# A hybrid recurrence and convolution block: the recurrent branch without GpSimd arithmetic, one-row products joined, the last filter layer stacked

## Chip, cores and metric

The kernel runs on one core of a Trainium2 chip. The metric is the device time of one execution in microseconds (us). Engines are named as the profile names them: PE (TensorE, products), PEld (its weight loads), DVE (VectorE), ACT (ScalarE), POOL (GpSimd), SP (DMA issue).

## The reference

One layer on 512 tokens of width 1024, in float32:

```
h   = x + Mixer(rmsnorm(x));  h = h + PEER(rmsnorm(h));  out = rmsnorm(h)
Mixer: proj = xn @ w_in, cut into q, zf_fwd, zf_bwd, inp, og, (x0, x1, v), gates
 A, 8 heads of 128: f = lb + (1-lb)*sigmoid(zf), k = (1-lb)*sigmoid(-zf), q = silu(q)
    S_t = diag(f_t) S_{t-1} + k_t inp_t^T,  o_t = S_t^T q_t   forward and reversed, summed
    y_a = (rmsnorm(o) * silu(og)) @ w_branch_a
 B, 1024 channels: width-3 convolution of x0, x1, v;  u = v*x1
    filters = (sin(sin(features) ...) @ filt_w3) * exp(-t*|decay|), forward and backward
    y_b = (x0 * (two-sided FFT convolution of u with the filters + bias*u)) @ w_branch_b
 out = (sigmoid(g_a)*y_a + sigmoid(g_b)*y_b) @ w_out
PEER: 8 heads choose 16 of 128^2 experts per token; sum of gelu(x.u_e)*g_e*v_e
```

## The kernel before

Float32 accuracy is had from fp32r products: an operand is split into `hi` (a cast by ACT, L85) and `lo = x - hi` (a subtraction, L86, on DVE unless the call names `nc.gpsimd`), and `mm3` issues hi*hi (L93), a product with the other operand's `lo` (L94) and one with its own (L95). `proj` loads 128 columns of a weight as `wraw` (128x1024), splits them into `whi` and `wlo`, two buffers, and sums 24 products of 512 columns in one of three PSUM banks `ps_mm`. Here L94 takes `xl, whi` and L95 takes `xh, wlo`.

The program has these stages: norm and turn of x to about 30 us; `hyena` to about 330, in four quarters of 256 channels; gates and projection of branch B to about 395; `hgrn`, 8 heads, to about 785; then `w_a`, `w_o` and PEER.

`hyena`: per quarter the projected rows are convolved, folded, transposed and split; the filter is made by two sine layers (once) and a last layer of 64 rows (`hid2`, `fw3`, L448, plain float32); both go through cosine and sine matrices as `mm3` sums (`ft`). The middle and the Nyquist element are single rows: `um`, `fm0`, `fm1` and `YN`, each as a hi and a lo tile of one row, enter a sum by two products with the row `alt` (L382 and L383, and others like them, 12 pairs in a quarter).

`hgrn`: `scores(hd)` scans the logarithms `lf` (L619) to `Z` on DVE (L628, L629), forms `EZ` and `E0` (L648 to L653), transposes `EZ` on PE (L662), builds the states `S`, and for 7 levels takes differences `Dt` (L689, L690), their exponential (ACT, L691), products `KM` (L692 to L694), a PE product (L698) and a masked copy into `sct` (L699). Beside it `weave` runs `project(hd+1)`: four projections, those with odd j split on POOL; then `sigmoids(hd+1)` and `values(hd+1)`, whose weights are split on POOL. Two more operations stand on POOL: `ksum` (L633) and the gating product of `so` (L621). The order within each engine comes from the framework's scheduler, not from the order of the code alone: each engine works its list in order, and a wait holds what stands behind it.

Of the kernel before, what the change touches and what calls it, by code (L numbers as in the profile page):

```python
# [21 lines left out]
P = 128  # L22
# [159 lines left out]
def turn(C, xn, xh, xl, tb):  # L182

    nc = C.nc
    ts_ = slice(tb * P, tb * P + P)
    for half in range(2):
        pt = C.ps_x.tile([P, 512], F32, name="ps_x")
        for j in range(4):
            k = half * 4 + j
            nc.tensor.transpose(pt[:, j * P : j * P + P], xn[:, k * P : k * P + P], C.ident)  # L190
        ks = slice(half * 4, half * 4 + 4)
        split(nc, xh[:, ks, ts_], xl[:, ks, ts_], pt.rearrange("p (j t) -> p j t", j=4))


FIRST_CONV = (8, 16)
# [107 lines left out]
def hyena(C, ctx, xh, xl, raws, fill):  # L303
# [9 lines left out]
    FH = 64  # L313
    NJ = HC // P
    H = L // 2

    first = dict(zip(FIRST_CONV, proj_halves(C, (None, None), xh, xl, raws=raws)))

# [5 lines left out]
        nc.vector.scalar_tensor_tensor(dst[:, : L - 1], ps[:, 1:], vcol(C, "cw2", blk), dst[:, : L - 1], op0=ALU.mult, op1=ALU.add)  # L324

    dft = {}
    hid2 = cp.tile([FH, L], F32, name="hid2")
    alt = cp.tile([1, H + 2], F32R, name="alt")
    altc = cp.tile([P, 1], F32R, name="altc")

    def setup(once):

        for name, w in (("ce", H + 2), ("so", H), ("co", H), ("se", H), ("coT", H), ("soT", H + 2)):
            hi = cp.tile([P, 2, w], F32R, name=name + "h")
            lo = cp.tile([P, 2, w], F32R, name=name + "l")
            for t in range(2):
                raw = once.tile([P, L], F32, name="dftraw", tag="ow", bufs=3)[:, :w]
                nc.sync.dma_start(raw, a[name][:, t])
                split(nc, hi[:, t], lo[:, t], raw)
            dft[name] = (hi, lo)  # L340
        raw = once.tile([P, L], F32, name="dftraw", tag="ow", bufs=3)
        nc.sync.dma_start(raw[:1, : H + 2], a["alt"])
        nc.sync.dma_start(raw[:, H + 2 : H + 3], a["altc"])
        nc.scalar.copy(alt, raw[:1, : H + 2])
        nc.scalar.copy(altc, raw[:, H + 2 : H + 3])


        zT = w2.tile([P, L], F32, name="zT", tag="x1")[:33]
        nc.sync.dma_start(zT, a["zT"])
        fw1 = once.tile([33, FH], F32, name="fw1")  # L350
        nc.sync.dma_start(fw1, a["f_w1"])
        fw2 = once.tile([FH, FH], F32, name="fw2")
        nc.sync.dma_start(fw2, a["f_w2"])

        def sine_layer(dst, ps, b, q):

            arg = once.tile([P, L], F32, name="arg", tag="ow", bufs=3)[:FH]
            kf = once.tile([P, L], F32, name="kf", tag="ow", bufs=3)[:FH]
            nc.vector.tensor_scalar(arg, ps, vcol(C, b)[:FH], vcol(C, q)[:FH], op0=ALU.add, op1=ALU.mult)
# [12 lines left out]
        ps = C.ps_x.tile([P, L], F32, name="ps_x")
        nc.tensor.matmul(ps[:FH], fw2, hid1, start=True, stop=True)
        sine_layer(hid2, ps[:FH], "f_b2", "f_q2")

    def ft(dst, mat, fb, src, mid=None):

        mh, ml = dft[mat]
        sl = slice(fb * P, fb * P + P)
        mm3(nc, dst, [((mh[:, t, sl], ml[:, t, sl]), (src[0][:, t], src[1][:, t])) for t in range(2)], stop=mid is None)  # L380
        if mid is not None:
            nc.tensor.matmul(dst, alt[:, sl], mid[0], start=False, stop=False)  # L382
            nc.tensor.matmul(dst, alt[:, sl], mid[1], start=False, stop=True)  # L383

    def nyquist(dst, src, mid):

        for t in range(2):
            nc.tensor.matmul(dst, altc, src[0][:, t], start=(t == 0), stop=False)
            nc.tensor.matmul(dst, altc, src[1][:, t], start=False, stop=False)
        nc.tensor.matmul(dst, alt[:, 0:1], mid[0], start=False, stop=False)  # L390
        nc.tensor.matmul(dst, alt[:, 0:1], mid[1], start=False, stop=True)

    def psum(w=HC):
        return C.ps_x.tile([P, L], F32, name="ps_x")[:, :w]
# [1 line left out]
    def hl(pool, shape, name, **kw):  # L396
        tag = kw.pop("tag", name)
        return (pool.tile(shape, F32R, name=name + "h", tag=tag + "h", **kw),
                pool.tile(shape, F32R, name=name + "l", tag=tag + "l", **kw))

    for half in range(D // HC):
        x0 = cp.tile([P, NJ, L], F32, name="x0")
        u = cp.tile([P, NJ, L], F32, name="u")
        us = hl(cp, [P, 2, HC], "us")
        ud = hl(cp, [P, 2, HC], "ud")
        um = hl(cp, [1, HC], "um")
        for j in range(NJ):
            cb = half * NJ + j
            x1 = w2.tile([P, L], F32, name="x1")
# [16 lines left out]
                split(nc, dst[0][:, :, js], dst[1][:, :, js], pt[:, q * HC : q * HC + HC].rearrange("p (t c) -> p t c", t=2))  # L426
            pm = psum(P)
            nc.tensor.matmul(pm[:1], uj[:, H : H + 1], C.ident, start=True, stop=True)
            split(nc, um[0][:, js], um[1][:, js], pm[:1])
            conv(x0[:, j], cb)  # L430
        if half == 0:
            with tc.tile_pool(name="hyo", bufs=1, side="right") as once:
                setup(once)

        fw3 = w2.tile([FH, 2, HC], F32, name="fw3", bufs=1)
        nc.scalar.dma_start(fw3, a["f_w3"].rearrange("f (d c) -> f d c", d=2)[:, :, half * HC : half * HC + HC])
        decb = w2.tile([P, 2, HC], F32, name="decb", bufs=1)
        for dr in range(2):
            o = dr * D + half * HC
            nc.scalar.dma_start(decb[:, dr], a["f_decay"][:, o : o + HC].to_broadcast([P, HC]))  # L440
        nc.scalar.activation(decb, decb, AF.Abs)
        pm_ = w2.tile([P, 2, 4, HC], F32, name="pm", bufs=1)
        for t in range(TB):
            win = w2.tile([P, 2, HC], F32, name="win")
            nc.scalar.activation(win, decb, AF.Exp, scale=vcol(C, "negt", t))
            ps = psum(2 * HC)
            for dr in range(2):
                nc.tensor.matmul(ps[:, dr * HC : dr * HC + HC], hid2[:, t * P : t * P + P], fw3[:, dr], start=True, stop=True)  # L448
            nc.vector.tensor_mul(win, ps.rearrange("p (d c) -> p d c", d=2), win)
            if t == 0:  # L450
                nc.vector.memset(win[0:1, 1], 0.0)
            nc.vector.tensor_add(pm_[:, 0, t], win[:, 0], win[:, 1])
            nc.vector.tensor_sub(pm_[:, 1, t], win[:, 0], win[:, 1])
        mid = []
        for q in range(2):
            m = hl(cp, [1, HC], f"fm{q}")
            split(nc, m[0], m[1], pm_[0:1, q, 2])
            mid.append(m)
        nc.vector.memset(pm_[0:1, :, 2], 0.0)
        fold = []  # L460
        for q in range(2):
# [82 lines left out]
def hgrn(C, ctx, xh, xl, ya, ga):  # L544
# [33 lines left out]
    def project(hd):  # L578

        raw = w2.tile([P, 4, L], F32, name="raw")  # L580
        for j, blk in enumerate((8 + hd, 16 + hd, hd, 32 + hd)):
            ps = proj(C, a["w_in"][blk], xh, xl, nc.gpsimd if j % 2 else None)
            nc.scalar.copy(raw[:, j], ps)
            yield
        st[hd] = [raw]

    def values(hd):
        ps = proj(C, a["w_in"][24 + hd], xh, xl, nc.gpsimd)
        vT = w1.tile([P, L], F32, name="vT")
        nc.scalar.copy(vT, ps)  # L590
        st[hd].append(vT)
# [747 lines left out]
```

## Time and profile before

| | |
|---|---|
| median of 3 runs | 2204.7 us (2198.98 to 2210.33) |
| profiled execution | 2201.49 us; span 2199.7; mean granted clock 0.989 |
| PE, DVE, ACT, POOL busy | 96%, 77%, 43%, 38% of the span |
| chain that ended last | PE 75%, DVE 15%, issue 5%, ACT 3%, DMA 1%, POOL 1% |

The shares of busy time are means over the stages named above, so each stage is read by its own window. PE is busy nearly throughout; ends of products are modelled, so the distance from one product's start to the next one's is the better measure of its price.

### The profile page before, as it was taken

To read this page: it belongs to the slowest core of one execution; us is meant where nothing else is said; L and a number is where in the kernel's file an instruction comes from. 1 tells how busy PE (TensorE), PEld (TensorE's weight loads), DVE (VectorE), ACT (ScalarE), POOL (GpSimd) and SP (SyncE) were. 2 spreads that over 40 slices of the span, in tenths; PEclk is the share of its full clock that TensorE was granted. 3 is DMA by queue.
4 is the path that set the end of the run, shared out by engine and by line. 5 is a ranking of instruction groups with operands and counts; after the bars stand their busy time and mean duration, and the time that the engine had idled before them with its cause. 6 is when DMAs were issued, how large, how long until landed. Compare 5 with 4: busy or idle time off the path is not lost.

```text
span 2199.7 us, 29965 instructions
## 1 busy us (share of the span) xinstructions
PE 2102.2 (96%) x11197; PEld 1842.4 (84%) x11197; DVE 1703.3 (77%) x2972; ACT 953.7 (43%) x1375; POOL 828.3 (38%) x452
## 2 busy tenths in 40 slices
PE   7999999999999999997989999999999999999998
PEld 6777778777777879877889889899898998899897
DVE  4677673678898773799999987877787887878874
ACT  5443442556565552323777533333332333333333
POOL 2101113222222231130000268777776667666650
PEclk9999999999999999998999999999999999999999
DMA  5211113212111244412645789889979978978964
GB/s 174 74 46 56 48 39 106 81 49 67 58 58 58 76 136 127 140 42 70 222 171 187 247 299 333 319 291 325 312 285 327 327 286 323 323 284 307 318 249 149
DMA packets 153084, 406.38 MB, mean 185 GB/s; under 512 B 12360, under 2 KB 64841, under 8 KB 151274
## 3 DMA queue, kind: packets, MB, share of 16 engines
q1 hardware_dynamic: 109882, 255.59, 34.5%
q0 software_dynamic: 36864, 134.23, 16.6%
q10 hardware_dynamic: 6192, 14.64, 2.1%
q8 instruction: 88, 1.44, 0.3%
q14 instruction: 58, 0.48, 0.1%
HBM read 372.30 MB, written 32.11 MB: 184 GB/s over the span
## 4 chain that ended last, share of the span: by engine, by line
PE 75%; DVE 15%; issue 5%; ACT 3%; DMA 1%; POOL 1%; DVEq 0%; ACTq 0%; POOLq 0%
PE acc L953 7%; PE acc L954 7%; PE acc L952 7%; PE ps_mm L95 7%; PE ps_mm L93 7%; PE ps_mm L94 7%; PE ps_a L95 7%; PE ps_a L93 7%; PE ps_a L94 7%; PE ps_g L1208 2%; PE ps_x L698 2%; PE ps_x L93 1%; PE ps_x L95 1%; PE ps_x L94 1%; DVE exp L1160 1%
## 5 line engine op out<-in xcount | busy, mean ns | idle before, releaser
L86 POOL TENSOR_TENSOR ul<-uraw,uh 128x1024 fp32r<-128x1024 f32 x100 | 259.7, 2597 | 470.2 <-ACT uh L85 466.5
L86 POOL TENSOR_TENSOR wlo<-wraw,whi 128x1024 fp32r<-128x1024 f32 x63 | 156.1, 2478 | 662.4 <-ACT whi L85 547.8
L85 ACT CAST vh<-vraw 128x1024 fp32r<-128x1024 f32 x128 | 134.7, 1052 | 530.9 <-DMA vraw<-in_v 476.9
L95 PE MATMUL ps_a<-pxh,ul 128*128 128x384 f32 x1008 | 343.1, 341 | 16.2 <-DVE ul L86 9.6
L93 PE MATMUL ps_a<-pxh,uh 128*128 128x384 f32 x1008 | 342.7, 340 | 3.3 <-ACT uh L85 1.8
L94 PE MATMUL ps_a<-pxl,uh 128*128 128x384 f32 x1008 | 340.5, 338 | 0.0
L954 PE MATMUL acc<-vh,gl 128*128 128x512 f32 x768 | 300.8, 392 | 0.0
L953 PE MATMUL acc<-vl,gh 128*128 128x512 f32 x768 | 300.6, 391 | 0.0
L952 PE MATMUL acc<-vh,gh 128*128 128x512 f32 x768 | 298.7, 389 | 0.0
L95 PE MATMUL ps_mm<-xh,wlo 128*128 128x512 f32 (+1 forms) x656 | 257.2, 392 | 6.4 <-POOL wlo L86 5.4
L93 PE MATMUL ps_mm<-xh,whi 128*128 128x512 f32 (+1 forms) x656 | 259.7, 396 | 0.1
L913 DVE SCALAR_TENSOR_TENSOR xg<-grow,gw,xg 128x1024 f32<-128x1024 f32 x127 | 199.9, 1574 | 76.8 <-DMA grow<-in_v,gidx 75.2
L94 PE MATMUL ps_mm<-xl,whi 128*128 128x512 f32 (+1 forms) x656 | 257.0, 392 | 0.0
L904 DVE SCALAR_TENSOR_TENSOR grow<-grow,xg 128x1024 f32<-128x1024 f32 x128 | 194.6, 1537 | 77.2 <-DMA grow<-in_u,gidx 77.1
L85 ACT CAST whi<-wraw 128x1024 fp32r<-128x1024 f32 x112 | 117.4, 1049 | 213.0 <-PE ps_mm L94 117.7
L95 PEld LDWEIGHTS ps_a<-pxh,ul 128*128 128x128 f32 x1008 | 190.9, 189 | 20.3 <-DVE ul L86 12.1
L884 POOL DMA_INDIRECT grow<-in_u,gidx x128 | 192.0, 1500 | 37.0 <-issue 21.4
L86 DVE TENSOR_TENSOR vl<-vraw,vh 128x1024 fp32r<-128x1024 f32 x128 | 188.8, 1479 | 13.7 <-ACT vh L85 13.7
L93 PEld LDWEIGHTS ps_a<-pxh,uh 128*128 128x128 f32 x1008 | 191.1, 190 | 8.8 <-ACT gact L845 2.6
L94 PEld LDWEIGHTS ps_a<-pxl,uh 128*128 128x128 f32 x1008 | 191.0, 190 | 3.7
L884 POOL DMA_INDIRECT grow<-in_v,gidx x128 | 170.4, 1332 | 36.6 <-issue 17.6
L954 PEld LDWEIGHTS acc<-vh,gl 128*128 128x128 f32 x768 | 144.1, 188 | 30.3
(423 smaller groups left out, 4311.8 us busy)
## 6 DMA issues: line engine op xcount, KB each, us to landing
uraw<-in_uT SPq DMA_DIRECT2D x128, 512.0 KB, 6.8
vraw<-in_v SPq DMA_DIRECT2D x128, 512.0 KB, 6.0
wraw<-in_w_in SPq DMA_DIRECT2D x80, 512.0 KB, 3.6
Gd<-Gs SPq DMA_DIRECT2D x12, 2048.0 KB, 7.4
gt<-Gd SPq DMA_DIRECT2D x32, 768.0 KB, 9.5
wraw<-in_w_q SPq DMA_DIRECT2D x16, 512.0 KB, 3.9
wraw<-in_w_b SPq DMA_DIRECT2D x8, 512.0 KB, 3.6
wraw<-in_w_a SPq DMA_DIRECT2D x8, 512.0 KB, 4.4
```

The costliest lines, as they stand in the source:

```text
L85: nc.scalar.copy(hi, src)
L86: return (eng or nc.vector).tensor_sub(lo, src, hi).ins
L93: nc.tensor.matmul(out, ah, bh, start=(i == 0), stop=False)
L94: nc.tensor.matmul(out, ah, bl, start=False, stop=False)
L95: nc.tensor.matmul(out, al, bh, start=False, stop=(stop and i == n - 1))
L698: nc.tensor.matmul(pl[:, cs], KM[:, 0, cs], KM[:, 1, cs], start=True, stop=True)
L884: nc.gpsimd.indirect_dma_start(out=t, out_offset=None, in_=tab, in_offset=bass.IndirectOffsetOnAxis(ap=gidx[:, j : j + 1], axis=0))
L904: nc.vector.scalar_tensor_tensor(t, t, 1.0, xg, op0=ALU.mult, op1=ALU.mult, accum_out=gdot[:, j : j + 1])
L913: nc.vector.scalar_tensor_tensor(gacc, t, gw[:, j : j + 1], gacc, op0=ALU.mult, op1=ALU.add)
L952: nc.tensor.matmul(acc[k][:, c], gh[:, ts_], vh[:, ds_], start=(r == 0), stop=False)
L953: nc.tensor.matmul(acc[k][:, c], gh[:, ts_], vl[:, ds_], start=False, stop=False)
L954: nc.tensor.matmul(acc[k][:, c], gl[:, ts_], vh[:, ds_], start=False, stop=(r == NK - 1))
```

## The change

In `hgrn` every operation on POOL is put on DVE: the splits of the projections with odd j, of the values and of the gates (28 splits of 128x1024), and 8 each of `so` and `ksum` (128x512). In `hyena` and in branch B's gates POOL keeps its splits. In `hyena` the two one-row tiles of a pair become rows 0 and 32 of one 33-row tile whose other rows are zero, `alt` stands in both rows, and one product takes the place of two (48 fewer). The last filter layer has `hid2` stacked as hi over lo on 128 rows; it is multiplied with `fw3h` (the same rows twice) in one product of 512 columns and, on the 64 hi rows, with `fw3l` in a second. Two ACT operations of the first quarter are held until the turned input is there.

```diff
+    def split_row(t, src):
+        nc.scalar.copy(t[0:1], src)
+        nc.vector.tensor_sub(t[LOW : LOW + 1], src, t[0:1])
-    hid2 = cp.tile([FH, L], F32, name="hid2")
-    alt = cp.tile([1, H + 2], F32R, name="alt")
+    hid2 = cp.tile([2 * FH, L], F32R, name="hid2")
+    alt = cp.tile([LOW + 1, H + 2], F32R, name="alt")
...
-        sine_layer(hid2, ps[:FH], "f_b2", "f_q2")
+        hid = w2.tile([P, L], F32, name="hid", tag="vv")[:FH]
+        sine_layer(hid, ps[:FH], "f_b2", "f_q2")
+        nc.scalar.copy(hid2[:FH], hid)
+        nc.vector.tensor_sub(hid2[FH:], hid, hid2[:FH])
...
         if mid is not None:
-            nc.tensor.matmul(dst, alt[:, sl], mid[0], start=False, stop=False)
-            nc.tensor.matmul(dst, alt[:, sl], mid[1], start=False, stop=True)
+            nc.tensor.matmul(dst, alt[:, sl], mid, start=False, stop=True)
...
+        for row in (0, FH):
+            nc.scalar.dma_start(fw3[row : row + FH], a["f_w3"].rearrange("f (d c) -> f d c", d=2)[:, :, half * HC : half * HC + HC])
+        fw3h = w2.tile([2 * FH, 2, HC], F32R, name="fw3h", bufs=1)
+        fw3l = w2.tile([FH, 2, HC], F32R, name="fw3l", bufs=1)
+        with tc.issue_after(C.turned):
+            nc.scalar.copy(fw3h, fw3)
+        nc.vector.tensor_sub(fw3l, fw3[:FH], fw3h[:FH])
...
-            for dr in range(2):
-                nc.tensor.matmul(ps[:, dr * HC : dr * HC + HC], hid2[:, t * P : t * P + P], fw3[:, dr], start=True, stop=True)
+            nc.tensor.matmul(ps, hid2[:, t * P : t * P + P], fw3h.rearrange("f d c -> f (d c)"), start=True, stop=False)
+            nc.tensor.matmul(ps, hid2[:FH, t * P : t * P + P], fw3l.rearrange("f d c -> f (d c)"), start=False, stop=True)
...
-            ps = proj(C, a["w_in"][blk], xh, xl, nc.gpsimd if j % 2 else None)
+            ps = proj(C, a["w_in"][blk], xh, xl)
...
-        ps = proj(C, a["w_in"][24 + hd], xh, xl, nc.gpsimd)
+        ps = proj(C, a["w_in"][24 + hd], xh, xl)
...
-        nc.gpsimd.tensor_mul(so[:, 1], raw[:, 3], so[:, 1])
+        nc.vector.tensor_mul(so[:, 1], raw[:, 3], so[:, 1])
...
-        nc.gpsimd.tensor_add(ksum, KQ[:, 0], KQ[:, 2])
+        nc.vector.tensor_add(ksum, KQ[:, 0], KQ[:, 2])
```

On DVE, before, where the levels of head 4 end and head 5 begins (`sct` is a level's masked copy, `Z` the first scan of head 5):

```order
L692 TENSOR_TENSOR KM<-KQ,Dt 128x512
L699 COPY_PREDICATED sct<-masks,ps_x 128x512
L693 TENSOR_TENSOR KM<-KQ,Dt 128x256
L694 TENSOR_TENSOR KM<-KQ,Dt 128x256
L86 TENSOR_TENSOR wlo<-wraw,whi 128x1024
L699 COPY_PREDICATED sct<-masks,ps_x 128x512
L620 SCALAR_TENSOR_TENSOR KQ<-raw,omlb,so 128x512
```

The same place after:

```order
L86 TENSOR_TENSOR wlo<-wraw,whi 128x1024
L710 TENSOR_TENSOR KM<-KQ,Dt 128x512
L711 TENSOR_TENSOR KM<-KQ,Dt 128x256
L712 TENSOR_TENSOR KM<-KQ,Dt 128x256
L717 COPY_PREDICATED sct<-masks,ps_x 128x512
L651 TENSOR_TENSOR ksum<-KQ 128x512
L638 SCALAR_TENSOR_TENSOR KQ<-raw,omlb,so 128x512
L639 TENSOR_TENSOR so<-raw,so 128x512
L646 SCALAR_TENSOR_TENSOR Z<-smask,lf 128x512
```

The split moved ahead of the last level's products, and `ksum` and `so` joined the list that ran without them.

On DVE, before, from the sums `tot` to the product `EZ` of head 5 (L652) that PE transposes next (`Dt` and `KM` belong to its first levels):

```order
L642 TENSOR_TENSOR tot<-Z,lf 128x4
L689 TENSOR_TENSOR Dt<-Z 128x8x64
L690 TENSOR_TENSOR Dt<-Z 128x8x64
L689 TENSOR_TENSOR Dt<-Z 128x16x32
L690 TENSOR_TENSOR Dt<-Z 128x16x32
L648 TENSOR_TENSOR EZ<-tot,Z 128x1024
L692 TENSOR_TENSOR KM<-KQ,Dt 128x8x64
L693 TENSOR_TENSOR KM<-KQ,Dt 128x4x64
L694 TENSOR_TENSOR KM<-KQ,Dt 128x4x64
L653 TENSOR_TENSOR E_5352<-KQ,E_5352 128x1024
L652 TENSOR_TENSOR EZ<-KQ,EZ 128x1024
```

After, from `tot` to the same product (now L670):

```order
L659 COPY tot<-Z 128x4
L86 TENSOR_TENSOR wlo<-wraw,whi 128x1024
L660 TENSOR_TENSOR tot<-Z,lf 128x4
L707 TENSOR_TENSOR Dt<-Z 128x8x64
L666 TENSOR_TENSOR EZ<-tot,Z 128x1024
L708 TENSOR_TENSOR Dt<-Z 128x8x64
L707 TENSOR_TENSOR Dt<-Z 128x16x32
L671 TENSOR_TENSOR E_5305<-KQ,E_5305 128x1024
L670 TENSOR_TENSOR EZ<-KQ,EZ 128x1024
```

One split and three differences stand ahead of the product now, where four differences and three level products stood.

On PE, before, in the middle levels of head 4 (`ps_x_5143` and `ps_x_5157` are level products, `ps_mm_5109` and `ps_mm_5169` the second and third projections of head 5):

```order
L93 MATMUL ps_mm_5109<-xh_86,whi_5105 128x512
L94 MATMUL ps_mm_5109<-xl_87,whi_5105 128x512
L95 MATMUL ps_mm_5109<-xh_86,wlo_5106 128x512
L698 MATMUL ps_x_5143<-KM_5136 128x128 x4
L698 MATMUL ps_x_5157<-KM_5150 128x128 x4
L93 MATMUL ps_mm_5169<-xh_86,whi_5165 128x512
L94 MATMUL ps_mm_5169<-xl_87,whi_5165 128x512
L95 MATMUL ps_mm_5169<-xh_86,wlo_5166 128x512
```

After (the same level products are `ps_x_5096` and `ps_x_5110`; `ps_mm_5062`, `ps_mm_5122` and `ps_mm_5182` are the second to fourth projections):

```order
L95 MATMUL ps_mm_5062<-xh_86,wlo_5059 128x512
L93 MATMUL ps_mm_5122<-xh_86,whi_5118 128x512
L716 MATMUL ps_x_5096<-KM_5089 128x128 x4
L94 MATMUL ps_mm_5122<-xl_87,whi_5118 128x512
L93 MATMUL ps_mm_5182<-xh_86,whi_5178 128x512
L716 MATMUL ps_x_5110<-KM_5103 128x128 x4
L94 MATMUL ps_mm_5182<-xl_87,whi_5178 128x512
L95 MATMUL ps_mm_5122<-xh_86,wlo_5119 128x512
L93 MATMUL ps_mm_5122<-xh_86,whi_5118 128x512
```

Products that need only `whi` were drawn ahead of the level products; the first one that needs the third projection's `wlo` now stands behind both of them.

## Rows read from the trace of the kernel before

**Rows 1.** The page's part 1: busy us, share of the span, instructions.

```profile
PE 2102.2 (96%) x11197; PEld 1842.4 (84%) x11197; DVE 1703.3 (77%) x2972; ACT 953.7 (43%) x1375; POOL 828.3 (38%) x452
```

**Rows 2.** Windows: convolution, recurrence, one head, a half-clock stretch.

```profile
core 0: us, PE busy (x) PEld busy (x) DVE busy (x) ACT busy (x) POOL busy (x), PEclk, DMA share, GB/s
40.00:400.00 360.00, 352.04 (x1796) 283.99 (x1796) 219.50 (x410) 146.78 (x260) 61.02 (x27) 1.00 0.22 65
400.00:785.00 385.00, 357.35 (x1932) 300.68 (x1930) 323.13 (x494) 223.53 (x278) 92.23 (x45) 0.98 0.20 61
663.90:707.90 44.00, 40.85 (x230) 34.36 (x229) 39.04 (x62) 26.92 (x33) 10.49 (x5) 1.00 0.19 60
415.90:419.30 3.40, 2.81 (x10) 2.53 (x11) 3.01 (x6) 0.97 (x2) 0.00 (x0) 0.50 0.00 0
```

**Rows 3.** Timeline of ACT: start us, duration us, operation; heads 0, 6, 7.

```profile
405.94 1.24 ACT L619 ACTIVATE lf<-sg,lbs,omlb 128x1024 f32<-128x1024 f32 x1
...
676.13 1.25 ACT L619 ACTIVATE lf<-sg,lbs,omlb 128x1024 f32<-128x1024 f32 x1
...
720.15 1.25 ACT L619 ACTIVATE lf<-sg,lbs,omlb 128x1024 f32<-128x1024 f32 x1
```

**Rows 4.** Waits, 385 to 825: waiter, releaser; total us, count, longest.

```profile
DVE wlo L86 <- ACT whi L85: 48.7, 12, 15.1
...
PE ps_x L662 <- DVE EZ L652: 18.9, 7, 4.1
...
PE ps_mm L95 <- POOL wlo L86: 5.4, 5, 1.1
```

**Rows 5.** Timeline of PE; in brackets idle us and releaser.

```profile
416.49 0.48 PE L662 MATMUL ps_x<-ident,EZ 128*128 128x128 f32 x1 [3.18 <-DVE EZ L652]
...
674.79 0.50 PE L95 MATMUL ps_mm<-xh,wlo 128*128 128x512 f32 x1 [1.07 <-POOL wlo L86]
...
689.38 0.30 PE L662 MATMUL ps_x<-ident,EZ 128*128 128x128 f32 x1 [2.07 <-DVE EZ L652]
```

**Rows 6.** Timeline of POOL, head 6.

```profile
681.03 2.37 POOL L86 TENSOR_TENSOR wlo<-wraw,whi 128x1024 fp32r<-128x1024 f32 x1 [4.06 <-ACT whi L85]
```

**Rows 7.** Timeline of DVE, heads 5 and 6.

```profile
657.61 0.68 DVE L690 TENSOR_TENSOR Dt<-Z 128x512 f32<-128x512 f32 x1
...
659.45 2.28 DVE L690 TENSOR_TENSOR Dt<-Z 128x512 f32<-128x512 f32 x1
...
673.28 2.54 DVE L86 TENSOR_TENSOR wlo<-wraw,whi 128x1024 fp32r<-128x1024 f32 x1 [4.02 <-ACT whi L85]
...
681.10 2.85 DVE L689 TENSOR_TENSOR Dt<-Z 128x512 f32<-128x512 f32 x1
...
688.02 1.21 DVE L652 TENSOR_TENSOR EZ<-KQ,EZ 128x1024 f32<-128x1024 f32 x1
...
694.58 1.23 DVE L86 TENSOR_TENSOR wlo<-wraw,whi 128x1024 fp32r<-128x1024 f32 x1 [0.37 <-PE ps_x L724]
```

**Rows 8.** Timeline of ACT, exponential of EZ in head 6.

```profile
685.72 1.06 ACT L650 ACTIVATE EZ<-EZ 128x1024 f32<-128x1024 f32 x1 [0.83 <-DVE EZ L648]
```

**Rows 9.** Timeline of PE in a transform.

```profile
107.49 0.38 PE L382 MATMUL ps_x<-umh,alt 1*128 1x256 f32 x1
107.72 0.27 PE L383 MATMUL ps_x<-uml,alt 1*128 1x256 f32 x1
107.92 0.39 PE L93 MATMUL ps_x<-udh,seh 128*128 128x256 f32 x1
```

**Rows 10.** Timeline of PE at the last filter layer.

```profile
78.66 0.39 PE L95 MATMUL ps_mm<-xh,wlo 128*128 128x512 f32 x1
78.89 0.39 PE L93 MATMUL ps_mm<-xh,whi 128*128 128x512 f32 x1
79.21 0.48 PE L448 MATMUL ps_x<-fw,hid 64*128 64x256 f32 x1
82.86 0.50 PE L94 MATMUL ps_mm<-xl,whi 128*128 128x512 f32 x1
```

More of the change, by code (lines that the diff above doesn't have):

```diff
@@ L191, in turn @@
         ks = slice(half * 4, half * 4 + 4)
-        split(nc, xh[:, ks, ts_], xl[:, ks, ts_], pt.rearrange("p (j t) -> p j t", j=4))
+        src = pt.rearrange("p (j t) -> p j t", j=4)
+        C.turned = nc.scalar.copy(xh[:, ks, ts_], src).ins
+        nc.vector.tensor_sub(xl[:, ks, ts_], src, xh[:, ks, ts_])
 FIRST_CONV = (8, 16)
@@ L315, in hyena, with one_row @@
     H = L // 2
+    LOW = 32
+    def one_row(name):
+        t = cp.tile([LOW + 1, HC], F32R, name=name)
+        nc.vector.memset(t.bitcast(F32), 0.0)
+        return t
+    def split_row(t, src):
+        nc.scalar.copy(t[0:1], src)
+        nc.vector.tensor_sub(t[LOW : LOW + 1], src, t[0:1])
     first = dict(zip(FIRST_CONV, proj_halves(C, (None, None), xh, xl, raws=raws)))
@@ L341, in setup @@
         raw = once.tile([P, L], F32, name="dftraw", tag="ow", bufs=3)
-        nc.sync.dma_start(raw[:1, : H + 2], a["alt"])
+        nc.vector.memset(raw[: LOW + 1, : H + 2], 0.0)
+        for row in (0, LOW):
+            nc.sync.dma_start(raw[row : row + 1, : H + 2], a["alt"])
         nc.sync.dma_start(raw[:, H + 2 : H + 3], a["altc"])
-        nc.scalar.copy(alt, raw[:1, : H + 2])
+        nc.scalar.copy(alt, raw[: LOW + 1, : H + 2])
         nc.scalar.copy(altc, raw[:, H + 2 : H + 3])
@@ L389, in nyquist @@
             nc.tensor.matmul(dst, altc, src[1][:, t], start=False, stop=False)
-        nc.tensor.matmul(dst, alt[:, 0:1], mid[0], start=False, stop=False)
-        nc.tensor.matmul(dst, alt[:, 0:1], mid[1], start=False, stop=True)
+        nc.tensor.matmul(dst, alt[:, 0:1], mid, start=False, stop=True)
     def psum(w=HC):
@@ L399, in hl @@
                 pool.tile(shape, F32R, name=name + "l", tag=tag + "l", **kw))
+    um, YN = one_row("um"), one_row("YN")
+    mid = [one_row(f"fm{q}") for q in range(2)]
     for half in range(D // HC):
@@ L405, in hyena @@
         ud = hl(cp, [P, 2, HC], "ud")
-        um = hl(cp, [1, HC], "um")
         for j in range(NJ):
@@ L428, in hyena @@
             nc.tensor.matmul(pm[:1], uj[:, H : H + 1], C.ident, start=True, stop=True)
-            split(nc, um[0][:, js], um[1][:, js], pm[:1])
+            split_row(um[:, js], pm[:1])
             conv(x0[:, j], cb)
@@ L433, in hyena @@
                 setup(once)
-        fw3 = w2.tile([FH, 2, HC], F32, name="fw3", bufs=1)
-        nc.scalar.dma_start(fw3, a["f_w3"].rearrange("f (d c) -> f d c", d=2)[:, :, half * HC : half * HC + HC])
+        fw3 = w2.tile([2 * FH, 2, HC], F32, name="fw3", bufs=1)
+        for row in (0, FH):
[5 more added lines that the diff above has]
+        nc.vector.tensor_sub(fw3l, fw3[:FH], fw3h[:FH])
         decb = w2.tile([P, 2, HC], F32, name="decb", bufs=1)
@@ L440, in hyena @@
             nc.scalar.dma_start(decb[:, dr], a["f_decay"][:, o : o + HC].to_broadcast([P, HC]))
-        nc.scalar.activation(decb, decb, AF.Abs)
+        with tc.issue_after(C.turned):
+            nc.scalar.activation(decb, decb, AF.Abs)
         pm_ = w2.tile([P, 2, 4, HC], F32, name="pm", bufs=1)
@@ L453, in hyena @@
             nc.vector.tensor_sub(pm_[:, 1, t], win[:, 0], win[:, 1])
-        mid = []
         for q in range(2):
-            m = hl(cp, [1, HC], f"fm{q}")
-            split(nc, m[0], m[1], pm_[0:1, q, 2])
-            mid.append(m)
+            split_row(mid[q], pm_[0:1, q, 2])
         nc.vector.memset(pm_[0:1, :, 2], 0.0)
@@ L514, in hyena @@
         nc.vector.tensor_mul(yn, un[:1], kN)
-        YN = hl(cp, [1, HC], "YN", tag="fm0")
-        split(nc, YN[0], YN[1], yn)
+        split_row(YN, yn)
         for j in range(NJ):
@@ L525, in hyena @@
             mm3(nc, pe, terms, stop=False)
-            nc.tensor.matmul(pe, YN[0][:, cs], alt, start=False, stop=False)
-            nc.tensor.matmul(pe, YN[1][:, cs], alt, start=False, stop=True)
+            nc.tensor.matmul(pe, YN[:, cs], alt, start=False, stop=True)
             po = psum(H)
@@ L603, in gates @@
         for db in range(KB):
-            ps = proj(C, a["w_in"][64 + db], xh, xl, nc.gpsimd if db % 2 else None)
+            ps = proj(C, a["w_in"][64 + db], xh, xl)
             nc.scalar.copy(ga[:, db], ps)
```

## The prediction

> **What bounds the kernel now.** I read the shares of the engines first, then windows by stage, then the waits, then the timelines around each wait. PE is busy 96% of the span and every other engine has slack as a mean [rows 1], so the only question is how much PE waits, or works for nothing, in the two stages that the change touches. By windows, the convolution from 40 to 400 has PE busy 352.04 of 360.00: 8.0 us of waiting at most, so time comes from there only by taking products away. The recurrence from 400 to 785 has 357.35 of 385.00: 27.6 us idle, and DVE at 323.1, 84% where the convolution has 61% [rows 2]. There a wait can be gained.
>
> The recurrence has a period. The logarithms of heads 0, 6 and 7 start at 405.94, 676.13 and 720.15 [rows 3]: 314.2 for seven heads, 44.9 on average, 44.02 for the last one. The six periods before take 270.2, 45.0 each. In the window of one late head PE is busy 40.85 of 44.00, DVE 39.04, POOL 10.49 with five operations (three splits, `ksum`, `so`) [rows 2]. The waits of the stage that PE has name two causes: 18.9 us in 7 waits for `EZ`, from DVE, and 5.4 in 5 for `wlo`, from POOL [rows 4]. In the late head they are single gaps, 2.07 and 1.07 [rows 5]: together 3.14, all of its 3.15 idle. In an early head the `EZ` gap is 3.18, and directly behind it lies a stretch of 3.4 us at a granted clock of 0.50, that is 1.2 GHz in place of 2.4 [rows 2, 5]: what PE did before the clock fell was wait.
>
> Why is `EZ` late? Its exponential on ACT waited 0.83 for DVE's subtraction [rows 8], and DVE had been stopped by POOL. The subtraction `Dt` takes 0.68 alone and 2.85 at 681.10, beside the POOL split that runs from 681.03 for 2.37 [rows 6, 7]. The same shows at 659.45 (2.28 in place of 0.68) and at 673.28 (a split, 2.54 in place of 1.23) [rows 7]. That is 2.17 + 1.60 + 1.31 = 5.1 us of DVE time per head that is blocking and no work.
>
> **The recurrence, part by part.** Moved to DVE per head: three splits at 1.23 and two operations of 128x512 at the 0.68 of `Dt` (a product of the same size), 3 x 1.23 + 2 x 0.68 = 5.05. Gone: the 5.1 of blocking. DVE's load stays at 39.0 per head, and POOL's 10.49 goes. So the change is free on DVE in sum; what counts is where in the list the operations stand.
>
> The wait for POOL's `wlo` (1.07) goes with POOL: on DVE the split takes 1.23 and not 2.37. What is late next: the order on PE shows the third projection's first product with `wlo` behind two level products, and DVE's list has the splits between level products and masked copies, so such a product can wait for a split behind another operation. The bounds are 0 (the products drawn ahead, which need only `whi`, cover it) and one split, 1.23; I take 0.7, a little over the middle.
>
> The wait for `EZ`: in DVE's list between `tot` and the product `EZ` one `Dt` (0.68), one `KM` of 512 (0.68, as `Dt`) and two of 256 (0.68 together, estimated as half each) and 2.17 of blocking leave, 4.2; one split of 1.23 enters. `EZ` comes 3.0 earlier after `lf`, while PE arrives 1.07 earlier: the gap of 2.07 + 1.07 - 3.0 would be 0.1. Bounds 0 and 2.07; since `ksum` and `so` now also stand ahead of the scans (1.4 us at most, if the logarithm does not cover them), I leave 0.45, about a quarter of that above 0.1. The new period is 44.02 - 3.15 + 0.7 + 0.45 = 42.0. Early heads lose their longer gap and the half clock behind it too, so seven periods go from 314.2 to 7 x 42.0 = 294.0: **-20.2**. Bounds: -28 where PE waits for nothing (7 x 40.87 = 286.1) and -6 where the late period stays for all heads (7 x 44.02 = 308.1). The gates' splits lie behind the last head and in its window; they move with the same balance and I cost them at nothing, hidden behind PE's products there; uncovered, four of them would cost 4 x 1.23 = 4.9.
>
> **The convolution.** One-row pairs: 12 a quarter, 48 in all, each losing one product. In the trace the two start 0.23 and 0.20 before what follows them (107.49, 107.72, 107.92) [rows 9]. The one that remains keeps the first price, so 48 x 0.20 = 9.6.
>
> Last filter layer: its products take 82.86 - 79.21 = 3.65 per quarter now [rows 10]. After it has eight of 512 columns. An ordinary one starts 0.23 after the one before (78.66, 78.89), and the first one of 64 rows 0.32 after a product of 128 rows [rows 10]; the new layer alternates between 128 and 64 rows, so each of the eight gets 0.32: 2.6, a gain of 1.1 and 4.4 in all. Bounds: 8 x 0.23 (gain 1.8, 7.2 in all), and 8 x 0.46, double price (nothing).
>
> Added: in the first quarter a cast on ACT and a subtraction on DVE behind the second sine layer (each estimated at half of the 1.23 that DVE's split of twice the columns takes [rows 7]: 1.2 together), per quarter a cast and a subtraction of `fw3`, two memsets, one more load. `fw3` is loaded and cast long before it is needed, beside the projections of the quarter, and PE has those products to issue meanwhile; so I cost these at nothing, and 1.2 for the sine chain, where PE has less to do. Bounds of what is added: 0, and 1.2 in each quarter plus as much as PE waits now once more, 4.8 + 8.0 = 12.8 against a gain of 14.0. I take 9.6 + 4.4 - 1.2 = **-12.8**, with -17 (9.6 + 7.2) and -1 as ends. Splits on POOL stay in this stage, 27 operations of 61.02 us [rows 2], so the blocking of DVE does not go here. The two operations held until the input is turned run before 40 us, in front of their use; nothing, or, if the filter waited for them, 1.
>
> **Sum.** 2201.5 (the profiled execution, 3.2 below the median of 2204.7 and inside the spread of the three runs) - 20.2 - 12.8 = **2168.5**, rounded to 2169. PEER and what lies around the span stay.
>
> **The rivals.** *DVE's list becomes the bound.* 39.0 of work in a period of 42.0 is 93%, in an engine that takes its list in order; at present it is 89% and still late at `EZ`. If each head has 2 us in which it waits for ACT or PE more than now, the period stays at 44.0: 314.2 - 308.0 = 6.2 gained, with the convolution's 12.8: 2182.5. For it: DVE waited 48.7 us for `whi` in 12 places of the stage already [rows 4]. Against it: the blocking that goes is of the same size as the work that comes, and most waits of DVE for ACT lie where it has nothing to do.
>
> *Slower: the splits wait on DVE.* A POOL split waits 4.06 for its cast, and holds nobody [rows 6]. On DVE the same wait holds the whole list; the splits there had waits of 48.7 / 12 = 4.06 on average [rows 4], one of 4.02 in the late head [rows 7]. If each of three moved splits had this, DVE would need 39.0 + 12.2 = 51.2 per head, 6.3 more than the 44.9 of now: 7 x 6.3 = +44, with the convolution 2201.5 + 44 - 12.8 = 2233. It decides as soon as these waits come to over 7.7 per head (44.9 + 12.8 / 7 - 39.0). Against it: on PE the new order issues products with the third and fourth projections' `whi` ahead of the first one with `wlo`, so these casts are done before the split is wanted.
>
> *PE waits for nothing.* DVE keeps ahead everywhere, -28, and the filter layer comes at its lower price, -17: 2156. For it speaks that the steady gaps have just the two causes that the change removes.
>
> *The second one-row product is nearly free.* Of 0.23, 0.20 and then 0.23 for the next ordinary product of 256 columns, which by half of the 0.23 of a 512-column one costs 0.12, some 0.1 may belong to the change of height that remains with one product. Then a removed product gives 0.12, 48 x 0.12 = 5.8, and the sum is 2172. The Trainium skill, in "TensorEngine Tiling (Array Packing)", Key Properties, says that a change of tiling mode drains TensorE; by that the price is the change's and not the product's, and the eight alternations of the filter layer pay it as well. The trace agrees on the filter's side (0.32 against 0.23) [rows 10], and for the rows it leaves both readings open.
>
> **How the numbers follow.** Forecast 0.62 (2169, its own range 2160 to 2184), DVE bound 0.18 (2183), slower 0.05 (2233), PE without waits 0.10 (2156), one-row products cheap 0.05 (2172). The range: below, 2156 less the convolution's 8.0 us of waiting, 2148, which I widen to 2145 as early heads may gain more by the clock; above, the ends -6 and -1 to -3 of both parts together, 2193. About 0.1 lies above it and 0.07 below. A measurement tells 0.5% from nothing here, that is 2193.7 and 2215.7 about the median. Slower: the 0.05. The same: the upper tail of the DVE case and of the forecast with its added waits, 0.08. Faster: 0.87.
>
> **What the profile after would show.** POOL without work between 400 and 785; `Dt` at 0.68 throughout and DVE busy near 39 per head; `lf` to `lf` 42.0, with the `EZ` gap under 1 and no half-clock stretch behind it; PE's wait for `wlo` now named with DVE. In the convolution 12 one-row products a quarter in place of 24, PE's starts 0.2 closer at each, and the filter layer's eight products in 2.6. Wrong would be: `lf` to `lf` at 44 or more, DVE waits for `whi` above 8 us per head, PE gaps at `EZ` that stay, or a filter layer that takes 3.6 again.

## The result and the profile after

The changed kernel takes 2176.14 us (median of 4, 2174.66 to 2176.48) against 2204.7: ratio 0.9866, 95% interval 0.9838 to 0.9894. The forecast was 2169 with a range of 2145 to 2193. The profiled execution has 2176.0 with a span of 2174.0. One execution of pool_memset (6926.9) and one of pad_both_dve (4231.72) took far longer than the others of the same kernel and are left out of the medians given below.

The page's part 1 and windows of the changed kernel, the first three as in [rows 1, 2], the last two around its half-clock stretches:

```profile
PE 2093.7 (96%) x11117; PEld 1829.3 (84%) x11117; DVE 1711.5 (79%) x3026; ACT 960.6 (44%) x1380; POOL 740.4 (34%) x408
```

```profile
40.00:400.00 360.00, 348.41 (x1720) 275.05 (x1719) 226.12 (x421) 149.13 (x265) 54.01 (x23) 0.99 0.22 67
...
569.50:611.40 41.90, 40.64 (x229) 34.26 (x229) 38.35 (x67) 27.25 (x33) 0.00 (x0) 1.00 0.22 64
187.60:191.00 3.40, 3.40 (x9) 2.69 (x10) 1.63 (x4) 0.62 (x3) 0.00 (x0) 0.56 0.39 149
208.30:211.60 3.30, 3.30 (x9) 2.57 (x10) 3.30 (x7) 1.08 (x3) 0.00 (x0) 0.53 0.03 7
```

Logarithms and the last sigmoid of the gates (ACT), PE's waits in the recurrence with those of head 4, and DVE on the way to `EZ` in head 4, all of the changed kernel:

```profile
404.58 1.25 ACT L637 ACTIVATE lf<-sg,lbs,omlb 128x1024 f32<-128x1024 f32 x1
443.54 1.25 ACT L637 ACTIVATE lf<-sg,lbs,omlb 128x1024 f32<-128x1024 f32 x1
...
569.45 1.25 ACT L637 ACTIVATE lf<-sg,lbs,omlb 128x1024 f32<-128x1024 f32 x1
611.41 1.25 ACT L637 ACTIVATE lf<-sg,lbs,omlb 128x1024 f32<-128x1024 f32 x1
...
695.35 1.24 ACT L637 ACTIVATE lf<-sg,lbs,omlb 128x1024 f32<-128x1024 f32 x1
...
761.24 3.62 ACT L267 ACTIVATE ga<-ga 128x4096 f32<-128x4096 f32 x1
```

```profile
PE ps_x L680 <- DVE EZ L670: 6.4, 7, 1.1
PE ps_mm L95 <- DVE wlo L86: 3.3, 8, 0.7
...
579.69 0.52 PE L680 MATMUL ps_x<-ident,EZ 128*128 128x128 f32 x3 [0.91 <-DVE EZ L670]
...
595.04 0.50 PE L95 MATMUL ps_mm<-xh,wlo 128*128 128x512 f32 x1 [0.35 <-DVE wlo L86]
```

```profile
573.04 1.22 DVE L86 TENSOR_TENSOR wlo<-wraw,whi 128x1024 fp32r<-128x1024 f32 x1
...
576.59 0.68 DVE L707 TENSOR_TENSOR Dt<-Z 128x512 f32<-128x512 f32 x1
...
578.33 1.22 DVE L670 TENSOR_TENSOR EZ<-KQ,EZ 128x1024 f32<-128x1024 f32 x1
```

The same sigmoid, and the half-clock stretch of the convolution, in the kernel before:

```profile
787.15 3.63 ACT L265 ACTIVATE ga<-ga 128x4096 f32<-128x4096 f32 x1
...
94.50:98.80 4.30, 4.30 (x14) 3.31 (x13) 4.18 (x5) 3.36 (x6) 2.69 (x1) 0.60 0.00 0
```

The period is 41.96 (569.45 to 611.41), 44.02 before [rows 3]. DVE does 38.35 in it, 39.04 before [rows 2], with no operation beside POOL. The waits of PE for `EZ` fell from 18.9 to 6.4, those for `wlo` from 5.4 to 3.3 [rows 4]. The four stretches at a granted clock of 0.50 that the recurrence had (from 415.9, 463.7, 511.5 and 555.9), each beginning at a wait of PE for `EZ`, are gone. The last sigmoid of the gates starts 25.9 earlier (761.24 for 787.15). The first logarithm starts only 1.4 earlier (404.58 for 405.94 [rows 3]): that is all the convolution gave. This figure is itself uncertain: with the new convolution the first logarithm lies between 403.95 and 404.90 in six of the runs below, and with the old one, in rec_only, at 407.43. PE in the convolution, the joined row and the filter layer:

```profile
108.37 0.28 PE L95 MATMUL ps_x<-ush,cel 128*128 128x256 f32 x1
108.58 0.38 PE L399 MATMUL ps_x<-um,alt 33*128 33x256 f32 x1
108.89 0.38 PE L93 MATMUL ps_x<-udh,seh 128*128 128x256 f32 x1
109.11 0.29 PE L94 MATMUL ps_x<-udl,seh 128*128 128x256 f32 x1
...
276.57 0.49 PE L471 MATMUL ps_x<-fw3l,hid 64*128 64x512 f32 x1
276.99 0.50 PE L470 MATMUL ps_x<-fw3h,hid 128*128 128x512 f32 x1
277.43 0.49 PE L471 MATMUL ps_x<-fw3l,hid 64*128 64x512 f32 x1
```

A joined row costs 0.31 (108.58 to 108.89), where the pair took 0.23 + 0.20 [rows 9]: 0.12 a pair, 5.8 in all. A filter product costs 0.42 to 0.44; by starts the layer takes 13.2 for 14.6 in four quarters. So 7.2 of product time went. New waits of PE, such as these, took half of it:

```profile
139.98 0.50 PE L93 MATMUL ps_mm<-xh,whi 128*128 128x512 f32 x1 [0.50 <-ACT whi L85]
141.89 0.50 PE L95 MATMUL ps_mm<-xh,wlo 128*128 128x512 f32 x1 [1.18 <-DVE wlo L86]
...
335.71 0.50 PE L95 MATMUL ps_mm<-yh,wlo 128*128 128x512 f32 x1 [1.78 <-DVE wlo L86]
```

PE's idle time from 40 to 400 grew from 8.0 to 11.6 (360.00 - 348.41), and there are two half-clock stretches where there was one (clock 0.60 over the window from 94.5 to 98.8). PE is busy all through them, so one more, of 3.4 us, is worth about 1.7. That is 7.2 - 3.6 - 1.7 = 1.9, near the 1.4 seen.

### The profile page after: what moved, and what is told of

Its sections match the earlier page's. It is cut to its first block, busy times and chain, and to the rows that moved or that the text cites. A ratio compares the mean times of both kernels' runs of the same rounds, so it can differ in the third digit from the quotient of the medians.

```text
span 2174.0 us, 29787 instructions
## 1 busy us (share of the span) xinstructions
PE 2093.7 (96%) x11117; PEld 1829.3 (84%) x11117; DVE 1711.5 (79%) x3026; ACT 960.6 (44%) x1380; POOL 740.4 (34%) x408
## 4 chain that ended last, share of the span: by engine, by line
PE 73%; DVE 15%; ACT 6%; issue 3%; DMA 2%; POOL 1%; ACTq 0%; DVEq 0%; POOLq 0%
PE acc L971 8%; PE acc L972 8%; PE acc L970 8%; PE ps_a L95 7%; PE ps_a L93 7%; PE ps_a L94 7%; PE ps_mm L94 6%; PE ps_mm L95 6%; PE ps_mm L93 6%; PE ps_g L1226 2%; PE ps_x L93 1%; PE ps_x L716 1%; PE ps_x L95 1%; PE ps_x L94 1%; DVE exp L1178 1%
## 5 line engine op out<-in xcount | busy, mean ns | idle before, releaser
L86 POOL TENSOR_TENSOR ul<-uraw,uh 128x1024 fp32r<-128x1024 f32 x100 | 264.7, 2647 | 461.0 <-ACT uh L85 460.0
L922 DVE SCALAR_TENSOR_TENSOR grow<-grow,xg 128x1024 f32<-128x1024 f32 x128 | 199.5, 1576 | 75.5 <-DMA grow<-in_u,gidx 75.3
L86 POOL TENSOR_TENSOR wlo<-wraw,whi 128x1024 fp32r<-128x1024 f32 x35 | 87.5, 2501 | 424.7 <-ACT whi L85 378.6
L86 DVE TENSOR_TENSOR vl<-vraw,vh 128x1024 fp32r<-128x1024 f32 x128 | 183.9, 1441 | 10.4 <-ACT vh L85 10.3
```

The lines of the kernel that those rows point to most:

```text
L922: nc.vector.scalar_tensor_tensor(t, t, 1.0, xg, op0=ALU.mult, op1=ALU.mult, accum_out=gdot[:, j : j + 1])
```

## The experiments

Each run is timed beside the kernel before, whose medians then are 2203.3 to 2207.9.

**rec_only**: the kernel before with the recurrence's lines of the diff alone, such as

```diff
-            ps = proj(C, a["w_in"][blk], xh, xl, nc.gpsimd if j % 2 else None)
+            ps = proj(C, a["w_in"][blk], xh, xl)
```

> The kernel before with only the recurrence's edits (splits, so and ksum on DVE); the convolution as before. Theory: nearly the whole gain of the change is the recurrence's. The logarithms run from head to head in 42.0 us instead of 44 to 45.8, and the end of the recurrence comes 24 to 26 us earlier: 2174 to 2181 us. Rival (the gain needs both edits, for instance a shorter convolution that lets DVE and the weights run ahead): 2183 to 2192.

2179.26, ratio 0.9894 (0.9861 to 0.9928). Period 42.0; the last sigmoid of the gates at 764.2, 23.0 earlier than before, as the first logarithm came 1.5 later (407.43). From the one to the other it is 356.8, as in the changed kernel (356.7): the recurrence needs nothing of the convolution's edits.

**hyena_only**: the changed kernel with all of the recurrence's lines put back.

```diff
-            ps = proj(C, a["w_in"][blk], xh, xl)
+            ps = proj(C, a["w_in"][blk], xh, xl, nc.gpsimd if j % 2 else None)
...
-        nc.vector.tensor_add(ksum, KQ[:, 0], KQ[:, 2])
+        nc.gpsimd.tensor_add(ksum, KQ[:, 0], KQ[:, 2])
```

> The kernel before with only the convolution's edits; the recurrence keeps its POOL work. Theory: products worth 7.1 us go (one-row pairs 0.43 to 0.31 each, 48 times; the filter layer 14.6 to 13.2 in all), and new waits of PE and a second half-clock stretch take 5 to 6 of them back: the first logarithm starts 0.5 to 3 us before 405.9 and the time is 2197 to 2203 us. Rival (the convolution's edits are worth the forecast 12.8, and the recurrence gave less than it seems): 2186 to 2192.

2203.12, ratio 1.0003 (0.9984 to 1.0022); first logarithm at 404.9. The convolution's edits give nothing that can be measured in the whole time.

**so_ksum_pool**

```diff
-        nc.vector.tensor_mul(so[:, 1], raw[:, 3], so[:, 1])
+        nc.gpsimd.tensor_mul(so[:, 1], raw[:, 3], so[:, 1])
```
and `ksum` likewise.

> The changed kernel with so and ksum back on POOL, splits on DVE; the order on PE, ACT and DVE is otherwise the same. Theory (a POOL operation that reads two operands stops DVE until it ends): DVE loses 16 operations of 0.68 and gets 16 holds of up to 1.3 to 2.1 each; ksum and so run where DVE comes to the scans that EZ waits for, so the EZ gap grows by 0.5 to 1 per head: 2178 to 2186 us. Rival (only the splits matter, the small operations are free wherever they stand): 2173 to 2177.

2176.79 (2175.32 to 2189.93), ratio 0.9895 (0.9845 to 0.9944). The rival is right: these 16 operations are free on either engine. My theory put them on the way to `EZ`, but PE waits there 6.4 in 7, as in the changed kernel. Over the seven periods DVE is busy for 260.2, 6.3 less than in the changed kernel (266.5), where 14 operations at 0.60 from start to start are 8.4: on POOL they hold DVE for some 2 us in all, an estimate, and not for 1.3 to 2.1 each.

**splits_pool**: the 28 splits back on POOL, for instance

```diff
-        ps = proj(C, a["w_in"][24 + hd], xh, xl)
+        ps = proj(C, a["w_in"][24 + hd], xh, xl, nc.gpsimd)
```

> The changed kernel with the 28 splits back on POOL, so and ksum on DVE; the scheduler then gives the recurrence the order of the kernel before. Theory: blocking and late wlo come back, 3 splits of 2.4 per head: period 43.5 to 45, end of the recurrence 16 to 24 us later: 2190 to 2200 us. Rival (so and ksum on POOL were what held DVE before the scans): 2176 to 2184.

2202.82, ratio 0.9998 (0.9975 to 1.002), later than expected. All of the gain is the 28 splits. The `EZ` wait is back, 20.1 us in 7, and so are four stretches of 3.4 us at a granted clock of 0.50 in the recurrence (from 461.5, 509.3, 553.7 and 686.8), one of them here:

```profile
461.50:464.90 3.40, 3.40 (x15) 3.00 (x14) 2.31 (x7) 0.73 (x2) 0.00 (x0) 0.50 0.00 0
```

PE is busy all through it, so the four are worth about 6.8, which my expectation left out.

**pool_idle**: the splits stay on DVE, and POOL gets work whose result nobody reads.

```diff
+            if j:
+                for q in range(2):
+                    nc.gpsimd.tensor_sub(idle, raw[:, j - q], xh[:, q].bitcast(F32))
```

> The changed kernel with six more POOL subtractions of 128x512 per head, whose result nobody reads; orders on PE, ACT and DVE are the same. Theory (blocking of DVE alone costs, nobody needs to wait for POOL): each holds DVE for up to 1.3 to 2 us, 8 or more per head against some 3.5 of slack of DVE (38.4 busy of 42.0), so the period grows to 43 to 47: 2184 to 2212 us. Rival (what cost before was only that wlo came late from POOL and the order): 2174 to 2178, and Dt at 0.68.

2193.7, ratio 0.9954 (0.9936 to 0.9972): 17.6 of the 28.6 are lost again, though nothing waits for POOL and the lists of the other engines are the same. Logarithms start 44.31 apart (579.27 and 623.58). The recurrence has no stretch at half clock in this run; what grew is PE's waits for DVE, from 9.7 in the changed kernel to 22.5 (385 to 785):

```profile
PE ps_mm L95 <- DVE wlo L86: 8.2, 8, 1.2
PE ps_x L684 <- DVE EZ L674: 7.2, 7, 1.5
PE ps_x L720 <- DVE KM L716: 7.1, 8, 1.4
```

**pool_memset** and **pool_memset_look**, one kernel; beside pool_idle:

```diff
-                    nc.gpsimd.tensor_sub(idle, raw[:, j - q], xh[:, q].bitcast(F32))
+                    nc.gpsimd.memset(idle, 0.0)
```

> As the run with six more POOL subtractions per head, but these write a constant and read nothing; same orders. Theory (the block is between POOL's reading and DVE's second operand): 2174 to 2178, Dt stays at 0.68. Rival (any work of POOL stops DVE): as long as with the subtractions.

> The run with six POOL writes of a constant per head once more, for its profile. Theory: period of the recurrence 42.0, Dt at 0.68 also beside POOL. Rival: Dt above 1 us beside POOL, period above 42.5.

2176.13 (median of four), and 2172.48 in pool_memset_look, a single execution, with a period of 42.0. The test was weak: with nothing to wait for, only 15 of 48 writes fell into the recurrence. Hence the next one.

**pool_memset_tied**

```diff
+            if j:
+                nc.gpsimd.tensor_sub(idle[:, 0:1], raw[:, j, 0:1], raw[:, j, 1:2])
+                for q in range(6):
+                    nc.gpsimd.memset(idle, 0.0)
```

> The changed kernel with POOL work of the amount of the run with six subtractions per head, at the places where those stood (behind the copies of three projections), but of constants written and not of operands read: 18 writes of 0.525 us per head behind a subtraction of one element per row that sets the place. Orders on PE, ACT and DVE are the same. Theory (what stops DVE is POOL's reading of operands): 2173 to 2178 us, period 42.0, Dt at 0.68 beside POOL. Rival (any work of POOL stops DVE): the period grows as with the subtractions, to 43.5 and more, 2185 to 2200.

2178.5, ratio 0.9862 (0.9834 to 0.9889). Groups by line from 400 to 770 (busy, mean ns, idle before), first with subtractions, then with writes:

```profile
L605 POOL TENSOR_TENSOR idle<-raw,xh 128x512 bf16<-128x512 f32 x44 | 69.5, 1579 | 243.2 <-ACT raw L602 241.5
...
L711 DVE TENSOR_TENSOR Dt<-Z 128x512 f32<-128x512 f32 x56 | 44.7, 799 | 0.0
```

```profile
L606 POOL MEMSET idle<- 128x512 bf16 x134 | 70.3, 524 | 7.8
...
L712 DVE TENSOR_TENSOR Dt<-Z 128x512 f32<-128x512 f32 x56 | 38.4, 685 | 0.0
```

POOL is as busy in both, 69.5 and 70.3. In the run with reads the same `Dt` takes 799 ns on average, in the run with writes 685, and there the period is 41.96 (569.09 to 611.05). Over the seven periods DVE is busy for 266.5 in the changed kernel, 266.6 with the writes and 292.9 with the reads, with the same list of operations in all three. What stops DVE is POOL reading operands.

**pad_rows**

```diff
-        t = cp.tile([LOW + 1, HC], F32R, name=name)
+        t = cp.tile([P, HC], F32R, name=name)
```
and `alt` likewise.

> The changed kernel with the joined rows' tiles and the row alt made 128 rows high (all others zero) instead of 33; the order on PE is the same. Theory (the price of the joined product, 0.31, is that of the change of height, twice over): a product of 128 rows costs what its neighbours do, 0.12, so 48 x 0.19 = 9.1 us of product time go; PE's waits may take a part back: 2165 to 2171 us. Rival (0.31 is the product's own price, whatever its height): 2175 to 2178.

2163.16, ratio 0.9826 (0.9792 to 0.9859); the first logarithm at 389.5, 15.1 before the changed kernel's. PE there:

```profile
108.98 0.28 PE L95 MATMUL ps_x<-ush,cel 128*128 128x256 f32 x1
109.10 0.28 PE L399 MATMUL ps_x<-um,alt 128*128 128x256 f32 x1
109.22 0.28 PE L93 MATMUL ps_x<-udh,seh 128*128 128x256 f32 x1
109.33 0.28 PE L94 MATMUL ps_x<-udl,seh 128*128 128x256 f32 x1
```

Three distances of about 0.12, 0.35 in all, stand where the 33-row product made 0.21 + 0.31 + 0.22 = 0.74: the change of height was paid ahead of the product and behind it too, which my expectation left out. Summed over all 48 places, the distances ahead of the joined product, at it and behind it fall from 34.5 to 17.5, by 17.0, of which 15.1 are seen; PE's waits from 40 to the first logarithm grow by 0.6 only (12.2 for 11.6).

**pad_fw**

```diff
-            nc.tensor.matmul(ps, hid2[:FH, t * P : t * P + P], fw3l.rearrange("f d c -> f (d c)"), start=False, stop=True)
+            nc.tensor.matmul(ps, hid2[:, t * P : t * P + P], fw3l.rearrange("f d c -> f (d c)"), start=False, stop=True)
```
with `fw3l` on 128 rows, the lower half zero.

> The changed kernel with fw3l made 128 rows high (its lower 64 zero) and multiplied with the whole stacked hid2; the order on PE is the same. Theory (the filter layer's 0.42 per product is the alternation between 128 and 64 rows): each of the 32 products costs 0.23 instead of 0.42, 6.1 us; if the half-clock stretch at 208 behind a filter layer also goes, 1.7 more: 2168 to 2172 us. Rival (0.42 is the price of reading hid2 or of another wait): 2175 to 2178, and the half-clock stretch stays.

2176.6 (2169.35 to 2181.77), ratio 0.988 (0.9839 to 0.9922). PE at the layer, then PE's waits from 40 to 400 (total, times, longest):

```profile
273.24 0.39 PE L471 MATMUL ps_x<-fw3h,hid 128*128 128x512 f32 x1
273.47 0.40 PE L472 MATMUL ps_x<-fw3l,hid 128*128 128x512 f32 x1
273.71 0.39 PE L471 MATMUL ps_x<-fw3h,hid 128*128 128x512 f32 x1
```

```profile
PE ps_x L93 <- ACT f0h L85: 3.4, 3, 1.5
...
PE ps_x L94 <- DVE f0l L86: 2.4, 1, 2.4
```

The price is as expected, 0.23, 6.1 less in all. The time is not: the first logarithm comes 2.9 earlier (401.7), and no gain of the whole run can be told from its spread. PE reaches the filter's transforms earlier and waits there for the folded filter, `f0l` 2.4 where the changed kernel had 1.0; all its waits from 40 to the first logarithm grow by 2.1, and those before 40 shrink by 1.9. The larger part went to the clock. The stretches at half clock before the first logarithm are three, 13.7 us for 6.8 in the changed kernel, worth 3.4 more. The longest of them begins while PE waits for `f0l`:

```profile
96.10 0.58 PE L94 MATMUL ps_x<-f0l,ceh 128*128 128x256 f32 x1 [2.43 <-DVE f0l L86]
...
95.80:102.60 6.80, 6.50 (x19) 5.28 (x20) 3.35 (x6) 3.11 (x5) 0.49 (x1) 0.50 0.17 61
```

6.1 - 2.1 + 1.9 - 3.4 = 2.5, near the 2.9 seen.

**pad_both**: the edits of pad_rows and pad_fw together, as

```diff
-    alt = cp.tile([LOW + 1, H + 2], F32R, name="alt")
+    alt = cp.tile([P, H + 2], F32R, name="alt")
...
-        fw3l = w2.tile([FH, 2, HC], F32R, name="fw3l", bufs=1)
+    fw3l = cp.tile([P, 2, HC], F32R, name="fw3l")
```

> The changed kernel with both kinds of zero rows: joined rows and alt on 128 rows, fw3l on 128 rows. Theory (product time falls by a further 6.1, but the first transforms of the filter wait for the fold on DVE and ACT, which come no earlier, as in the run with fw3l alone, whose recurrence ended 2.8 earlier and not 6.1): 2158 to 2163 us. Rival (with the rows shortened too, PE meets the filter's fold still earlier and all of the 6.1 is given back): 2162 to 2166.

2159.63 (2154.54 to 2162.89), ratio 0.9797 (0.9759 to 0.9835), first logarithm at 385.8, 3.7 before that of pad_rows. The time is that of the theory, though it cannot be told from the 2161.88 to 2165.35 of pad_rows. The theory's reason is a small part of it: PE's waits to the first logarithm grow by 0.8 over pad_rows (13.0 for 12.2), and the stretches at half clock before it are 13.7 us for 6.8 again, worth 3.4, which the expectation left out.

**pad_both_dve**: with both, the last POOL splits ahead of PEER taken away too.

```diff
-        ps = first.pop(blk, None) or proj(C, a["w_in"][40 + blk], xh, xl, nc.gpsimd if blk % 2 else None)
+        ps = first.pop(blk, None) or proj(C, a["w_in"][40 + blk], xh, xl)
```
and so in `proj_halves`, `gates_b`, the splits of `yb` and `ya`, and `w_b`.

> As the run with both kinds of zero rows, and all splits of the convolution, of branch B's gates and of the two output projections on DVE too, so that POOL has no arithmetic before 760. Theory (blocking of DVE by POOL holds the fold, the spectra and the sums that PE waits for there as well: 19.4 us of DVE time between 20 and 400 in the changed kernel): a third to a half of it is on the path: 2150 to 2158 us. Rival (DVE has 28 us more work in the convolution, 23 splits of 1.22, and takes them in order ahead of the chain that PE waits for): 2160 to 2170.

2141.79 (median of three), ratio 0.9719 (0.9671 to 0.9768): it beats both kernels, by 62 and by 34. From 40 to the first logarithm, in the changed kernel, in pad_both and in this run:

```profile
40.00:404.58 364.58, 352.99 (x1740) 278.86 (x1739) 228.63 (x424) 153.01 (x270) 54.01 (x23) 0.99 0.22 67
...
40.00:385.82 345.82, 332.82 (x1739) 276.13 (x1738) 228.66 (x423) 152.74 (x268) 54.30 (x23) 0.98 0.23 71
...
40.00:369.38 329.38, 323.14 (x1730) 270.19 (x1729) 233.29 (x445) 151.01 (x267) 0.00 (x0) 1.00 0.24 73
```

DVE took over 23 operations of POOL, 19 of 128x1024 and 4 of 128x512, which at 1.13 and 0.60 from start to start are 23.9, and is busy for only 4.6 more than in pad_both (233.29 for 228.66). So some 19 us of blocking went with them, an estimate from these figures and the amount that the theory had. PE waits for 6.2 in place of 13.0, at full clock throughout, and the first logarithm starts 16.4 earlier (369.38). That is more than the theory had: 6.8 of waits, and 13.7 us at half clock, worth another 6.8, went together. The order on PE changed too, so this run doesn't separate the blocking from the order.

## Why the prediction was right or wrong

The time lay in the range, 7 above the forecast, by two misses of opposite sign.

**The recurrence: right in mechanism, undersized.** Forecast -20.2. From the first logarithm to the last sigmoid of the gates the kernel needs 356.66 for 381.21 before: -24.6. `EZ` follows the logarithm by 8.88 (569.45 to 578.33) where it was 11.89 (676.13 to 688.02 [rows 3, 7]): the 3.0 that the prediction had added up from DVE's list. The period came as worked out (41.96 for 42.0), and so did what remains of the two waits: 0.9 for `EZ` and 0.35 for `wlo` per head, 1.25 where 1.15 was taken, though 0.7 and 0.45 the other way round. The first head was mis-sized: 38.96 (404.58 to 443.54) in place of 42.0, which I had assumed for all seven; why it is shorter stays open. The seven periods gave 23.4 (314.2 to 290.8), and 1.1 came behind the last logarithm, where the prediction had put the gates' splits at nothing. DVE's sum held, 38.35 for 39.0. That POOL's reads block DVE, and that this alone costs time, is shown by pool_idle against pool_memset_tied, in which the lists of PE, ACT and DVE are the same. pool_idle gives back 17.6, splits_pool all. Of what lies between, the four stretches at half clock of splits_pool are worth about 6.8; `wlo` late from POOL and the other order were not separated.

**`so` and `ksum`** I counted as part of the balance. They are no part of the gain.

**The convolution: wrong.** Forecast -12.8, measured -1.4. Three steps failed. "The one that remains keeps the first price, so 48 x 0.20": the joined product got dearer, 0.31, and the gain was 0.12 a pair; that is the size that the rival of the nearly free second product gave, 5.8. The Trainium skill says in "TensorEngine Tiling (Array Packing)", Key Properties, that changing the tiling mode drains TensorE. The prices here agree with it, 0.74 with a change of height against 0.35 without; the drain itself stands in no row. "Each of the eight gets 0.32": 0.42, since the 0.32 came from a single change and the alternation pays on both sides; 1.4 in place of 4.4. And the waits, taken at 1.2, were 3.6, with 1.7 of half clock. Why the waits grew is shown for one of them: at the last (335.71) PE came to `yh, whi` 3.2 earlier than before (333.19 for 336.35), and DVE began this `wlo` only 1.3 earlier (333.35 for 334.62). For the others it stays open, and earlier arrival alone is not the rule: pad_rows takes 17.0 more from the products of this stage, and its waits grow by 0.6. hyena_only shows the sum of the three, pad_rows and pad_fw the first two.

**The rivals.** DVE didn't become the bound. The waits of the splits for ACT did not come: DVE waits for no `whi` in the seven periods, where the kernel before had 26.5. The time was nearest to the rival of 2172. Its price for the pairs was the right one; its 9.0 for the whole convolution was still too large, and what brought the sum near was the recurrence's surplus of 4.4, which is luck.

## What to carry to other kernels

An engine off the critical path can hold another one by reading: look for one operation with two durations, and for what runs on POOL beside the longer one. A product of few rows among full ones can cost more than a full one (0.31 for 0.12 here, and twice more at its neighbours); here zero rows gave that back. Time taken from PE counts only as far as the next result of another engine lets PE go on, and a wait that it leaves can cost a second time by the clock behind it (pad_fw).

## What the hardware showed that I had not expected

A 128-row product with 126 rows of zeros takes 0.12, the same with 33 rows 0.31. POOL's writes, 70.3 us of them, lengthened nothing on DVE (685 ns), its reads did (799 ns). The half-clock stretch at 208.3 had no wait of PE before it: it stands directly behind eight filter products that alternate between 128 and 64 rows. These products aren't enough to bring it: hyena_only, splits_pool, so_ksum_pool, pool_idle and pool_memset_tied have the same ones in the same convolution and no stretch behind them, but near 40, 188, 290 and 334. What sets the place stays open.
